# An encoder layer by Strassen-like products: w_ada blocks in turn, weights asked for ahead, other rings, and right output columns kept on chip

## The chip, the cores and the metric

One core of a Trainium2 chip (8 cores) runs the kernel. Its engines are TensorE (PE; its weight loads are PEld), VectorE (DVE), ScalarE (ACT), GpSimd (POOL) and SyncE (SP). Transfers are issued here by SP and POOL (a few at the start by ACT) and carried out by 16 DMA engines. The metric is the device time of one execution in microseconds; lower is better.

## What is computed

One layer of a bidirectional encoder on x of 1024 x 2048 (float32):

```python
mod = jax.nn.silu(c) @ w_ada + b_ada                 # w_ada 2048 x 6144
shift, scale, gate = jnp.split(mod, 3, axis=-1)
h = rmsnorm(x, pre_g) * (1.0 + scale[:, None]) + shift[:, None]
proj = h @ w_in                                      # 2048 x 4608
q, k, v, gate_a, u, gate_p = jnp.split(proj, SPLIT_POINTS, axis=-1)
y_a = windowed_gqa(q, k, v, rel_table, sink) * jax.nn.silu(gate_a)
y_p = multiscale_pool(u, w_pool_grp, pool_scale) * jax.nn.silu(gate_p)
g = jax.nn.sigmoid(h @ w_merge + b_merge)            # 2048 x 4096
g_a, g_p = jnp.split(g, N_BRANCHES, axis=-1)
merged = g_a * (y_a @ w_br_attn) + g_p * (y_p @ w_br_pool)
o = merged @ w_out                                   # 2048 x 2048
return x + gate[:, None] * rmsnorm(o, post_g)
```

## The kernel before

**Products.** A float32 factor is split into a high part (ACT, line 91) and a low part (DVE, line 92), and a product is three matmuls: high by high, high by low, low by high. Blocks of 256 weight columns by 1024 rows of x are multiplied by a seven-product scheme of the Strassen-Winograd kind (`strassen`, line 199). One such unit, a *pair* below, has seven steps; with four row tiles a step is 12 matmuls of 128x512, with two (in the ramp) it is 6. `product` issues the matmuls (line 223), `prep` splits the weights, DVE forms the sums of weights in `raw` tiles, and ACT and DVE take the banks X, Z and V out. Raw weights come as two tiles of a ring of four, loaded by `load_raws` (line 178) at the opening of the pair's generator. `run` (line 306) drives one pair through its steps; the last step of a pair is issued at step 2 of the next one (`flush`), and *side steps* from a queue are hung between the steps (`placed`, line 94: behind the last matmul and the last low part).

**Order.** The program is built by a framework that keeps dependencies, places tiles in memory and fixes the order of every engine's instructions ahead of the run; each engine and each DMA queue then runs its own list in that order, waiting where something is not there yet.

**Stages.** (1) *Start* (lines 331 to 533): x is loaded and its rows normed and transposed; w_ada is used in blocks of 256 columns. Blocks 0 and 1 are loaded by SP and 2 and 3 by POOL (`ada_slots`, line 407; 16 tiles of 256 KB each), their column sums are formed on PE (`modulation`, lines 415 and 427), and each fills one row tile of the moving operands (`fill_steps`, line 478). (2) *Ramp* (lines 535 to 555): six pairs with the first two row tiles, then the same six with the other two; blocks 2 and 3 are side steps from numbers 4 and 15, their fills from 12 and 27. (3) *First pass* (`pass1`, line 559): the remaining pairs with the first half of K. The first 19 carry side steps at 4 of 7 steps: the rest of w_ada (`modulation_steps`, `gate_step`), sums of w_out's tiles for the last stage (`weight_sums`), the gate row by eight row sums (`gate_row`, line 599), and last the lines of the attention bias (`bias_lines`, line 583), which end in a 2 MB copy in DRAM on POOL's queue. The other nine carry x's second half at 5 of 7 steps (`x_step`, line 698): load by POOL, scaling by ACT (line 686), transposes by PE (line 692), and more weight sums. x and weight sums share a ring of eight tiles (`x_tile`, line 679). (4) *Second pass*: 34 pairs with the second half of K, with attention and pooling at their side. (5) *Branches* (line 979): 16 pairs. (6) *Last stage* (lines 1050 to 1344): merged @ w_out by the same scheme in four blocks of seven products of 48 matmuls (line 1102). Blocks 0 and 1 use the first half of K and store their results to `po_d`; 2 and 3 use the second half, load them back and add. Block 2 (left columns of each half) stores its weighed results to `o_d`, which the end loads again as `orow`; in `finish_rows` (line 1285) a row's scale is formed and 32 tiles are written out, nine of them by scaling on ACT and a transfer that adds x in place, the others by one DVE instruction each (line 1298).

```python
        queue(tiles[kc], w_ada[...])                                # ada_slots, 411
        raws = raws or load_raws(w, n0, row0, js)                   # strassen, 209
        side.insert(100, bias_lines)                                # 665: the list has 75 entries
```

Of the kernel before, what the change touches and what calls it, by code (L numbers as in the profile page):

```python
# [42 lines left out]
def encoder_layer(ctx: ExitStack, tc: tile.TileContext, x, c, table, w_ada, b_ada, pre_g,  # L43
# [95 lines left out]
    o_d = dram.tile([S, D // 2], F32, name="o_d")  # L139
# [59 lines left out]
    def strassen(w, n0, row0, js, op, finish, part=None, raws=None, swap=False):  # L199
# [9 lines left out]
        raws = raws or load_raws(w, n0, row0, js)  # L209
# [89 lines left out]
    late, evs = [], [None]  # L299
# [6 lines left out]
    def run(gen, side=None, every=(0, 2, 4, 6), at=None, then=None):  # L306
# [224 lines left out]
    for tag in SEEDED:  # L531
        hi = op["B11"][0][0]
        nc.tensor.matmul(bank(tag, "OPEN"), hi[:, 0:P], hi, start=True, stop=True)

    def ramp_pair(jj, i, parts, at):
# [3 lines left out]
        if ahead < 2 * RAMP:  # L539
            raws.append(load_raws(*weight_of(ORDER[ahead % RAMP]), 0, ((0, 1), (2, 3))[ahead // RAMP]))  # L540
        run(strassen(w, n0, 0, (2 * jj, 2 * jj + 1), op, to_dram(dst), parts, raws[jj * RAMP + i]),
            side, range(7), at)

    parts = {}
# [52 lines left out]
    gsum = {}  # L597

    def gate_row(n):
        if n < 8:  # L600
            gsum[n] = bank("at")
            nc.tensor.matmul(gsum[n][0:1, 0:256], ones, gacc[:, n * 256:(n + 1) * 256],
                             start=True, stop=True)
        n -= 1
        if n < 0:
            return
        sl = slice(n * 256, (n + 1) * 256)
        grow = gp.tile([1, 3, 256], F32, tag="grow", name=uid("grow"))
        side_load(grow[:, 0, :], b_ada[0:1, 2 * D + n * 256:2 * D + (n + 1) * 256])
        side_load(grow[:, 1, :], post_g[0:1, sl])  # L610
        add(grow[:, 2, :], gsum.pop(n)[0:1, 0:256], grow[:, 0, :])
        nc.vector.tensor_tensor(grow[:, 2, :], grow[:, 2, :], grow[:, 1, :], ALU.mult)
        side_store(pg_d[:, sl], grow[:, 2, :])
# [50 lines left out]
    side.extend(lambda n=n: gate_row(n) for n in range(9))  # L664
    side.insert(100, bias_lines)
# [13 lines left out]
    def x_tile():  # L679
        return sp.tile([P, 512], F32, tag="xt2", name=uid("xt"), bufs=8)  # L680
# [17 lines left out]
    def x_step(n):  # L698
        if n < 2 * NB:
            held[n] = fetch_x(n // 2, n % 2)  # L700
        if n >= 2:
            turn_x((n - 2) // 2, n % 2, held.pop(n - 2))

    steps = [lambda n=n: x_step(n) for n in range(2 * NB + 2)]
    steps += [lambda k=k, s=s: modulate((nc.scalar, nc.vector)[s], h[k][s], k) for k in h for s in range(2)]
    side = deque(with_sums(steps, 2, 4, range(8, 16), x_tile))
# [340 lines left out]
    def mslot(name, dt=F32, shape=(P, 512)):  # L1047
# [8 lines left out]
    queue = deque((q, w) for q in range(4) for _, w in ORDERS[q])  # L1056
# [20 lines left out]
    def prep_wo():  # L1077
# [4 lines left out]
        for src in loaded.popleft():  # L1082
            if not queue and not loaded:
# [29 lines left out]
    def out_sums(q, banks, fetch_op):  # L1113

        i = q % 2
        bx, bz = banks

        def copied(name, ps):
            for t in range(4):
                r = ev.tile([P, 512], F32, tag="pv", name=uid("c"), bufs=2)  # L1120
                nc.scalar.activation(r, ps[t], AF.Copy)
                store(at_rows(po_d, name, t, i), r)

        def summed(name, r, ps):
            for t in range(4):
                add(r[t], ps[t], r[t])
                store(at_rows(po_d, name, t, i), r[t])
# [6 lines left out]
        u2 = four("ev")  # L1134
# [7 lines left out]
        u3 = four("gt")  # L1142
# [41 lines left out]
    def put_later(n):  # L1184
# [4 lines left out]
        for j in range(KS):  # L1189
            t = mslot("lm")  # L1190
# [19 lines left out]
    for j in range(KS):  # L1210
        put(op, "T2", j, mt2[j])
        sub(m_t[2 * j, 0], mt2[j], m_t[2 * j, 0])
    out_sums(0, new_banks(0), first_fetch)
    out_sums(1, new_banks(1), put_later)
# [8 lines left out]
    parts, rows_x, rows_o = {}, {}, {}  # L1223

    def fetch_sums(i, blk):
        parts[blk] = [mslot("po") for _ in range(4)]
        for t in range(4):
            load(parts[blk][t], at_rows(po_d, blk, t, i))
# [6 lines left out]
    def weigh(i, blk, r):  # L1235
        nc.vector.tensor_tensor(r, r, pgrow[int(blk[0]) - 1][:, i * 512:(i + 1) * 512], ALU.mult)

    def take(i, blk, ps, r):

        for t in range(4):  # L1240
            add(r[t], ps[t], r[t])
            squares(i, blk, t, r[t])
            weigh(i, blk, r[t])
            if i == 0:
                store(at_rows(o_d, blk, t, 0), r[t])
# [4 lines left out]

    bx, bz = new_banks(2)
    fetch_sums(0, "12")
    product("B11", bx, True)
    for t in range(4):
        nc.scalar.activation(bz[t], bx[t], AF.Copy)
    fetch_sums(0, "11")
    product("T2", bz, False)
    seeded(bz, parts["12"])
    fetch_sums(0, "22")
    product("B21", bx, False)  # L1260
    take(0, "11", bx, parts["11"])
    product("T3", bz, False)
    seeded(bz, parts["22"])
    fetch_sums(0, "21")
    product("T1", bx, True)
    take(0, "22", bx, parts["22"])
    product("T4", bz, False)
    take(0, "21", bz, parts["21"])
    product("B22", bx, False)
    take(0, "12", bx, parts["12"])  # L1270

    def by_dma(half, t, n):
        return n in (0, 2) if half == 0 else n == 0 and t == 0

    def fetch_rows(half, t):
        si = half * 4 + t
        rows_x[si] = [None if by_dma(half, t, n) else slot("xr", F32) for n in range(4)]
        rows_o[si] = [slot("orow", F32) for _ in range(2)]
        for n in range(2):
# [103 lines left out]
```

## Time and profile before

| | |
|---|---|
| median of 3 runs | 2195.38 us (2192.98 to 2196.26) |
| the profiled execution | 2197.48 us, its span 2195.6 us |
| mean granted TensorE clock | 0.985 |
| HBM read, written | 329.92 MB, 142.63 MB |
| DMA packets' share of 16 engines, SP's queue | 53.9% |
| the same, POOL's queue | 11.6% |

The span runs from the first to the last instruction of one profiled execution, and all durations below are from it. A row of an engine's timeline has start and duration in us, the engine, the line of the kernel, the operation, output <- inputs, and how many instructions are merged; in brackets stands the idle time before it and what ended that. A row of a stretch has busy time and count of PE and PEld (and of DVE, ACT and POOL where no line is chosen), then granted clock, share of the DMA engines and GB/s. SPq, POOLq are the queues' issuing instructions.

### The profile page before, as it was taken

To read this page: it belongs to the slowest core of one execution; us is meant where nothing else is said; L and a number is where in the kernel's file an instruction comes from. 1 tells how busy PE (TensorE), PEld (TensorE's weight loads), DVE (VectorE), ACT (ScalarE), POOL (GpSimd) and SP (SyncE) were. 2 spreads that over 40 slices of the span, in tenths; PEclk is the share of its full clock that TensorE was granted. 3 is DMA by queue.
4 is the path that set the end of the run, shared out by engine and by line. 5 is a ranking of instruction groups with operands and counts; after the bars stand their busy time and mean duration, and the time that the engine had idled before them with its cause. 6 is when DMAs were issued, how large, how long until landed. Compare 5 with 4: busy or idle time off the path is not lost. (4 is left out here: it accounts for less than half of the span.)

```text
span 2195.6 us, 29101 instructions
## 1 busy us (share of the span) xinstructions
PE 2102.8 (96%) x9613; PEld 1714.9 (78%) x9613; DVE 1500.3 (68%) x2699; ACT 1088.8 (50%) x2015; POOL 179.8 (8%) x388
## 2 busy tenths in 40 slices
PE   5799999999999789999999999999999999999996
PEld 3478888877777568888888888788888788788884
DVE  6478777766444596777776777865867977655557
ACT  5464443433345554677667433333645645545344
POOL 2201232221201400000000000000000000000001
PEclk9799999999999999999999999999999999999998
DMA  9658778875445855554654576675754646898498
GB/s 332 220 201 271 254 271 271 270 264 172 146 140 156 289 197 188 174 175 149 204 171 144 180 227 202 206 240 173 243 165 160 218 134 203 258 330 265 156 316 270
DMA packets 280392, 472.42 MB, mean 215 GB/s; under 512 B 25898, under 2 KB 122258, under 8 KB 280240
## 3 DMA queue, kind: packets, MB, share of 16 engines
q1 hardware_dynamic: 252880, 386.22, 53.9%
q0 software_dynamic: 27024, 84.28, 11.6%
q8 instruction: 76, 1.25, 0.2%
q14 instruction: 76, 0.62, 0.1%
q10 hardware_dynamic: 336, 0.06, 0.0%
HBM read 329.92 MB, written 142.63 MB: 215 GB/s over the span
## 5 line engine op out<-in xcount | busy, mean ns | idle before, releaser
L91 ACT ACTIVATE whi<-raw 128x512 fp32r<-128x512 f32 (+1 forms) x540 | 320.8, 600 | 507.6 <-PE Z L223 235.0
L92 DVE TENSOR_TENSOR wlo<-raw,whi 128x512 fp32r<-128x512 f32 (+1 forms) x540 | 348.8, 652 | 148.9 <-PE Z L223 110.6
L102 DVE TENSOR_TENSOR raw<-raw,raw 128x512 f32<-128x512 f32 x78 | 54.0, 692 | 117.7 <-DMA raw<-in_w_merge_dram 68.4
L92 DVE TENSOR_TENSOR wlo<-wr,whi 128x512 fp32r<-128x512 f32 x112 | 76.3, 688 | 63.4 <-ACT whi L91 63.4
L91 ACT ACTIVATE whi<-wr 128x512 fp32r<-128x512 f32 x112 | 69.6, 627 | 98.9 <-PE OUT L1102 94.3
L223 PE MATMUL V<-T3h,whi 128*128 128x512 f32 x336 | 95.1, 400 | 6.0 <-DVE u L102 5.9
L223 PE MATMUL X<-B11h,whi 128*128 128x512 f32 x336 | 93.2, 395 | 7.0 <-ACT B11h L91 4.0
L223 PE MATMUL Z<-T2h,whi 128*128 128x512 f32 x336 | 93.4, 396 | 4.4 <-ACT whi L91 3.7
L223 PE MATMUL Z<-T2h,wlo 128*128 128x512 f32 x336 | 92.8, 394 | 3.4 <-DVE wlo L92 3.4
L223 PE MATMUL X<-B11l,whi 128*128 128x512 f32 x336 | 92.7, 392 | 2.5 <-DVE B11l L92 2.5
L223 PE MATMUL Z<-T1h,whi 128*128 128x512 f32 x336 | 94.1, 395 | 1.0 <-ACT T1h L91 0.8
L223 PE MATMUL V<-T3h,wlo 128*128 128x512 f32 x336 | 92.4, 395 | 1.6 <-DVE wlo L92 1.6
L223 PE MATMUL Z<-B22h,whi 128*128 128x512 f32 x336 | 92.3, 393 | 1.4 <-ACT u L272 1.4
L223 PE MATMUL V<-T4h,whi 128*128 128x512 f32 x336 | 92.3, 392 | 0.7 <-ACT T4h L91 0.7
L223 PE MATMUL V<-T3l,whi 128*128 128x512 f32 x336 | 92.9, 395 | 0.0
L223 PE MATMUL Z<-B22h,wlo 128*128 128x512 f32 x336 | 91.0, 390 | 1.9 <-DVE wlo L92 1.9
L223 PE MATMUL Z<-T2l,whi 128*128 128x512 f32 x336 | 92.7, 394 | 0.0
L223 PE MATMUL X<-B21h,wlo 128*128 128x512 f32 x336 | 91.1, 390 | 1.2 <-DVE wlo L92 1.2
L223 PE MATMUL Z<-T1l,whi 128*128 128x512 f32 x336 | 92.2, 392 | 0.0
L223 PE MATMUL X<-B11h,wlo 128*128 128x512 f32 x336 | 91.8, 391 | 0.0
L223 PE MATMUL V<-T4h,wlo 128*128 128x512 f32 x336 | 91.1, 390 | 0.5 <-DVE wlo L92 0.5
L223 PE MATMUL X<-B21h,whi 128*128 128x512 f32 x336 | 91.6, 392 | 0.0
(360 smaller groups left out, 5034.4 us busy)
## 6 DMA issues: line engine op xcount, KB each, us to landing
part<-part_d SPq DMA_DIRECT2D x136, 256.0 KB, 4.6
raw<-in_w_merge_dram SPq DMA_DIRECT2D x64, 512.0 KB, 5.0
raw<-in_w_in_dram SPq DMA_DIRECT2D x60, 512.0 KB, 4.4
ada<-in_w_ada_dram POOLq DMA_DIRECT2D x96, 256.0 KB, 5.7
proj_d<-part SPq DMA_DIRECT2D x68, 256.0 KB, 2.2
gada<-in_w_ada_dram POOLq DMA_DIRECT2D x32, 512.0 KB, 6.1
gt<-proj_d SPq DMA_DIRECT2D x64, 256.0 KB, 3.6
wr<-ws_d SPq DMA_DIRECT2D x32, 512.0 KB, 5.7
```

Source lines behind the costliest of these rows:

```text
L91: nc.scalar.activation(hi, src, AF.Copy)
L92: return nc.vector.tensor_tensor(lo, src, f32(hi), ALU.subtract)
L102: (eng or nc.vector).tensor_tensor(o, a, b, ALU.add)
L223: last_mm[0] = nc.tensor.matmul(ps, w_[:, i], op[mov][j][m_], start=fresh and i == 0 and n == 0, stop=i == nj - 1 and n == 2, skip_group_c ...
```

## The change

1. *Start.* A small POOL instruction (`mark`) reads tile 13 of block 1, and the loads of blocks 2 and 3 are put behind it on POOL. Ten opening matmuls (five a bank, before one a bank) stand between the sums of block 1 and its fill, before at the end of both fills. In the ramp, blocks 2 and 3 are side steps from 10 and 19 (one a step, and every second step), the fill of block 2 from 14.
2. *Weights.* `run` asks for the raw weights of the next full pair at its step 3 (`fetch_weights`) from a list of all pairs to come; `strassen` takes what was loaded.
3. *Gate row and bias.* The gate's sums are 16 products of one column each, then one transpose and two DVE instructions; its vectors are loaded at once, with the bias lines, at step 9 of the first part of the first pass. That part has 18 pairs, so x comes in ten.
4. *Rings.* x and weight sums have four tiles each of their own; x is transposed three steps after its load instead of two.
5. *Last stage.* The blocks run in the order 0, 1, 3, 2. Block 1 keeps its 16 result tiles on chip, in the ring that held the merged input, and block 3 adds to them and keeps them to the end; the tiles through which the second operand is read move to another ring. `o_d`, the adding transfers and the second trip of the right columns fall away. Partial results of block 0 and x come by POOL's queue. The products T4 and T1 of the final block run row by row as B22 did, the weights of the last but one product have slots of their own, rows are finished from T4 on, and the seed of B22 is added before it.

```diff
-    late, evs = [], [None]
+    late, evs, fetched, wanted_w = [], [None], deque(), deque()
+
+    def fetch_weights():
+        if wanted_w:
+            fetched.append(load_raws(*wanted_w.popleft(), range(4)))
...
-        raws = raws or load_raws(w, n0, row0, js)
+        raws = raws or fetched.popleft()
...
+            if i == 3 and ahead:
+                fetch_weights()
...
-    ada += [ada_slots(m, side_load) for m in (2, 3)]
+    mark = const.tile([P, 1], F32, name="mark")
+    come = ada[1][KT - 3][:, 0, 0:1]
+    with tc.issue_after(nc.gpsimd.tensor_tensor(mark, come, come, ALU.add).ins):
+        ada += [ada_slots(m, side_load) for m in (2, 3)]
     for m in range(2):
         all_of(modulation(m, ada[m]))
+        if m == 1:
+            for tag in SEEDED * 5:
+                hi = op["B11"][0][0]
+                nc.tensor.matmul(bank(tag, "OPEN"), hi[:, 0:P], hi, start=True, stop=True)
         all_of(fill_steps(m))
     claim((2, 3))
     side = deque([lambda: None] * (7 * RAMP))
-    for m, g0, f0 in ((2, 4, 12), (3, 15, 27)):
+    for m, g0, f0 in ((2, 10, 14), (3, 19, 27)):
         for n, f in enumerate(modulation(m, ada[m])):
-            side[g0 + 2 * n] = f
+            side[g0 + (m - 1) * n] = f
...
+    wanted_w.extend((*weight_of(n0), 0) for n0 in ORDER[RAMP:])
+    wanted_w.extend((*weight_of(n0), HALF * P) for n0 in ORDER)
+    wanted_w.extend((w, n * 256, 0) for w in (w_ba, w_bp) for n in range(8))
...
+    def gate_columns():
+        pg = bank("at")
+        for k in range(KT):
+            nc.tensor.matmul(pg[:, k:k + 1], gacc[:, k * P:(k + 1) * P], ones, start=True, stop=True)
+        nc.vector.tensor_copy(gcol, pg[:, 0:KT])
...
-    side.extend(lambda n=n: gate_row(n) for n in range(9))
-    side.insert(100, bias_lines)
+    side.extend((gate_columns, gate_row))
+    side.insert(9, lambda: (fetch_gate_row(), bias_lines()))
...
-        return sp.tile([P, 512], F32, tag="xt2", name=uid("xt"), bufs=8)
+        return sp.tile([P, 512], F32, tag="xt2", name=uid("xt"), bufs=4)
+
+    def sum_tile():
+        return sp.tile([P, 512], F32, tag="ws2", name=uid("wsum"), bufs=4)
...
+    BLOCKS = (0, 1, 3, 2)
...
-            if not queue and not loaded:
+            if len(queue) + len(loaded) == 1:
                 hi, lo = slot("whi"), slot("wlo")
...
-            t = mslot("lm")
+            t = ev.tile([P, 512], F32, tag=("gt", "ev")[n % 2], name=uid("lm"), bufs=4)
...
-    out_sums(1, new_banks(1), put_later)
+    out_sums(1, new_banks(1), put_later, kept)
...
     def finish_rows(half, t):
...
-            if by_dma(half, t, n):
-                nc.scalar.activation(o_[n], o_[n], AF.Copy, scale=s_[:, 2:3])
-                nc.gpsimd.dma_start(o_[n], x[at], accum_op=ALU.add)
...
+        for n in (1, 3, 2, 0):
+            o_ = (last, kept)[n % 2][f"{n // 2 + 1}{half + 1}"][t]
+            nc.vector.scalar_tensor_tensor(o_, o_, s_[:, 2:3], rows_x[si][n], op0=ALU.mult, op1=ALU.add)
+            store(out[si * P:(si + 1) * P, n * 512:(n + 1) * 512], o_)
...
-    product("T4", bx, False)
...
+    product("T4", bx, False, by_rows=True)
+    for t in range(2):
+        fetch_rows(1, t)
     for t in range(4):
+        squares(0, "21", t, bx[t])
+        weigh(0, "21", last["21"][t], bx[t])
+        finish_rows(0, t)
+    product("T1", bz, False, by_rows=True)
+    for t in range(2, 4):
         fetch_rows(1, t)
...
+        squares(0, "22", t, bz[t])
+        weigh(0, "22", last["22"][t], bz[t])
+        add(bz[t], bz[t], last["12"][t])
     product("B22", bz, False, by_rows=True)
     for t in range(4):
...
+        squares(0, "12", t, bz[t])
+        weigh(0, "12", last["12"][t], bz[t])
         finish_rows(1, t)
```

More of the change, by code (lines that the diff above doesn't have):

```diff
@@ L304, in flush, with run @@
             next(late.pop())
-    def run(gen, side=None, every=(0, 2, 4, 6), at=None, then=None):
+    def run(gen, side=None, every=(0, 2, 4, 6), at=None, then=None, ahead=True):
         for i in range(7):
@@ L595, in bias_lines, with gate_row, fetch_gate_row @@
               bass.AP(line_d.tensor, line_d.offset, [[LINE, NH], [0, P], [1, LINE]]))
[L597 to L613, printed above, removed]
+    grow = gp.tile([KT, 4, P], F32, name="grow")
+    gcol = gp.tile([P, KT], F32, name="gcol")
+    def gate_columns():
[3 more added lines that the diff above has]
+        nc.vector.tensor_copy(gcol, pg[:, 0:KT])
+    def gate_row():
+        pt = bank("at")
+        nc.tensor.transpose(pt[0:KT, 0:P], gcol, ident)
+        add(grow[:, 2], pt[0:KT, 0:P], grow[:, 0])
+        nc.vector.tensor_tensor(grow[:, 3], grow[:, 2], grow[:, 1], ALU.mult)
+        side_store(pg_d.rearrange("a (r p) -> (a r) p", p=P), grow[:, 3])
+    def fetch_gate_row():
+        side_load(grow[:, 0], b_ada[0, 2 * D:3 * D].rearrange("(r p) -> r p", p=P))
+        side_load(grow[:, 1], post_g[0].rearrange("(r p) -> r p", p=P))
     def weight_sums(n, tile_):
@@ L1055, in encoder_layer @@
     SETS = (("sc", "sc", "at", "at"), ("mm", "mm", *SEEDED))
-    queue = deque((q, w) for q in range(4) for _, w in ORDERS[q])
+    queue = deque((q, w) for n, q in enumerate(BLOCKS) for _, w in ORDERS[n])
     loaded, ready = deque(), deque()
@@ L1111, in at_rows, with out_sums, tiles, done @@
         return d[r0:r0 + P, n0:n0 + 512]
[L1113 to L1115 removed]
+    def out_sums(i, banks, fetch_op, keep=None):
         bx, bz = banks
+        def tiles(tag):
+            return four(tag) if keep is None else [mslot("po") for _ in range(4)]
+        def done(name, t, r):
+            if keep is None:
+                store(at_rows(po_d, name, t, i), r)
+            else:
+                keep.setdefault(name, []).append(r)
         def copied(name, ps):
             for t in range(4):
[L1120 removed]
+                r = ev.tile([P, 512], F32, tag="pv", name=uid("c"), bufs=2) if keep is None else mslot("po")
                 nc.scalar.activation(r, ps[t], AF.Copy)
[L1122 removed]
+                done(name, t, r)
         def summed(name, r, ps):
@@ L1133, in out_sums @@
         product("T2", bz, False)
-        u2 = four("ev")
+        u2 = tiles("ev")
         for t in range(4):
@@ L1141, in out_sums @@
         product("T3", bz, False)
-        u3 = four("gt")
+        u3 = tiles("gt")
         for t in range(4):
@@ L1249, in seeded, with opening, ev_tile @@
             add(r[t], ps[t], r[t])
-    bx, bz = new_banks(2)
[L1252 to L1261, printed above, removed]
+    def opening(banks, r12, then):
+        bx, bz = banks
+        product("B11", bx, True)
+        for t in range(4):
+            nc.scalar.activation(bz[t], bx[t], AF.Copy)
+        then()
+        product("T2", bz, False)
+        seeded(bz, r12)
+        product("B21", bx, False)
+    def ev_tile(tag):
+        return ev.tile([P, 512], F32, tag=tag, name=uid("po"), bufs=4)
+    bx, bz = new_banks(2)
+    opening((bx, bz), kept["12"], lambda: None)
+    take(1, "11", bx, kept["11"])
     product("T3", bz, False)
-    seeded(bz, parts["22"])
-    fetch_sums(0, "21")
+    seeded(bz, kept["22"])
+    fetch_sums("12", lambda: ev_tile("ev"))
+    fetch_sums("11", lambda: ev_tile("gt"))
     product("T1", bx, True)
-    take(0, "22", bx, parts["22"])
+    take(1, "22", bx, kept["22"])
     product("T4", bz, False)
-    take(0, "21", bz, parts["21"])
+    take(1, "21", bz, kept["21"])
     product("B22", bx, False)
-    take(0, "12", bx, parts["12"])
-    def by_dma(half, t, n):
-        return n in (0, 2) if half == 0 else n == 0 and t == 0
+    take(1, "12", bx, kept["12"])
     def fetch_rows(half, t):
         si = half * 4 + t
-        rows_x[si] = [None if by_dma(half, t, n) else slot("xr", F32) for n in range(4)]
-        rows_o[si] = [slot("orow", F32) for _ in range(2)]
-        for n in range(2):
-            load(rows_o[si][n], o_d[si * P:(si + 1) * P, n * 512:(n + 1) * 512])
+        rows_x[si] = [slot("xr", F32) for _ in range(4)]
         for n in range(4):
-            if rows_x[si][n] is not None:
-                load(rows_x[si][n], x[si * P:(si + 1) * P, n * 512:(n + 1) * 512])
+            side_load(rows_x[si][n], x[si * P:(si + 1) * P, n * 512:(n + 1) * 512])
     def finish_rows(half, t):
```

74 lines of the change are left out of this document (22 added, 52 removed).

## The prediction

> **What bounds the kernel now.** I read the page first: its busy times and TensorE's row of tenths over 40 slices.
>
> ```profile
> span 2195.6 us, 29101 instructions
> PE 2102.8 (96%) x9613; PEld 1714.9 (78%) x9613; DVE 1500.3 (68%) x2699; ACT 1088.8 (50%) x2015; POOL 179.8 (8%) x388
> ...
> PE   5799999999999789999999999999999999999996
> ```
>
> TensorE bounds nearly all of it. It is short of full in three places: the first two slices, the slices around 760 us and the last one. A busy share hides smaller holes, so I counted the products' own matmuls (line 223) in stretches, and took the pitch of a full product from the chain of waits.
>
> ```profile
> 1588.30 2.72 PE V L223 x12
> 640.00:680.00 40.00, 40.00 (x178) 33.12 (x177) 1.00 0.37 111
> 440.00:640.00 200.00, 189.59 (x812) 153.17 (x811) 0.98 0.57 186
> 680.00:840.00 160.00, 134.06 (x544) 102.38 (x543) 0.97 0.68 226
> ```
>
> Twelve matmuls in 2.72 us are 0.227 us each; an undisturbed stretch has 178 in 40 us. At that rate 440 to 640 should hold 890 and 680 to 840 should hold 712. Missing are 78 (17.7 us) and 168 (38 us). These two holes, the start and the end are what the change can win; elsewhere TensorE runs at its pitch or the change doesn't reach, and what it saves there on other engines or in transfers is worth nothing.
>
> **The start.** Block 1 of w_ada (16 tiles, SP queue) shares the transfers with blocks 2 and 3 on POOL.
>
> ```profile
> 0.74 22.02 SPq L355 DMA_DIRECT2D xt<-in_x_dram  x32
> 36.74 23.82 SPq L411 DMA_DIRECT2D ada<-in_w_ada_dram  x16
> 39.22 5.95 POOL L411 DMA_DIRECT2D ada<-in_w_ada_dram  x8 [0.61 <-PE GEMV L427]
> 50.97 0.69 DVE L92 TENSOR_TENSOR B22l<-XT,B22h 128x512 fp32r<-128x512 f32 x1
> 68.22 0.42 DVE L432 COPY acc<-GEMV 128x256 f32<-128x256 f32 x1 [14.52 <-PE GEMV L427]
> xt<-in_x_dram SPq DMA_DIRECT2D x32, 256.0 KB, 5.4
> 79.34 1.22 PE L223 MATMUL Z<-T2h,whi 128*128 128x512 f32 x2 [0.67 <-ACT Z L249]
> 84.20 0.91 PE L223 MATMUL X<-B21h,whi 128*128 128x512 f32 x2
> ```
>
> Alone, x tiles of the same 256 KB went out every 22.02/32 = 0.69 us; the 16 tiles of block 1 took 23.82/16 = 1.49 us each. With blocks 2 and 3 held back behind the mark, 16 x 0.69 = 11 us of issue and 5.4 us to land put the last tile at 53 us and the copy of its sums near 54, now 68.2. DVE has finished the operands of block 0 at 51.7 and then stands until those sums come, so nothing else is late before 54: the first products come **14 us** earlier. Bounds: 10 (the raw weights issued behind block 1 are late, or what follows) and 15 (DVE is then the limit). Blocks 2 and 3 now start near 51; their 32 issues at 0.69 us end some 22 us later, and later still beside the stores: near 80. The side steps that need them move from 4 and 15 to 10 and 19; at 6 x 0.227 = 1.36 us a step after a start near 64 that is 78 and 90, and each block is taken over four steps. They just fit; if not, PE stands in order before such a step.
>
> The ten opening matmuls stand in PE's order between the sums and the first product, where it waits for operands anyway. From 79.34 to 84.20, 11 matmuls ran at 0.44 us each, twice the pitch; at 0.227 they would save 2.4 us. The ten could warm the clock in that gap: from 0 to 2.4, I take 1.5.
>
> The Trainium skill, "TensorE: Matmul & The Clock Gate", section "What's actually happening", says that the full clock comes after a busy window of about 3.4 us, and that the windows run free of the kernel. By that rule ten matmuls of 0.44 us fill one window or none, and this term would be 2.4 or 0; the 0.44 agrees with its half clock.
>
> **The gate row.** Eight sums of two matmuls over 256 columns become 16 of one column and one transpose.
>
> ```profile
> 532.71 1.07 PE L223 MATMUL X<-B21h,wlo 128*128 128x512 f32 x4
> 533.71 0.59 PE L602 MATMUL b<-gacc,ones 128*1 128x256 f32 x2
> 534.24 1.20 PE L223 MATMUL V<-T4h,whi 128*128 128x512 f32 x4
> 535.27 1.08 PE L223 MATMUL V<-T4l,whi 128*128 128x512 f32 x4
> 41.54 1.08 PE L396 MATMUL PM<-ones,acc 128*128 128x1 f32 x8
> ```
>
> From 532.71 to 535.27 pass 2.56 us for eight matmuls worth 1.82: one group costs 0.74, eight cost 5.9. The new sums have the form of line 396, 1.08 us for eight: 2.2 for 16, and about 0.5 for the transpose. Saved **3.2** (2 to 4). The small loads on POOL become two and come early; the bias lines take their memset, two loads, matmuls, copy and two stores with them to step 9, at the same cost on PE. The first pass is one pair shorter and the second one longer.
>
> **Weights ahead.** Two stalls stand in the same hole.
>
> ```profile
> 474.67 1.28 DVE L578 SCALAR_TENSOR_TENSOR gacc<-gada,sc,gacc 128x1024 f32<-128x1024 f32 x1 [3.03 <-DMA gada<-in_w_ada_dram]
> 480.55 0.69 DVE L105 TENSOR_TENSOR ws<-raw 128x512 f32<-128x512 f32 x1 [3.39 <-DMA raw<-in_w_merge_dram]
> 481.89 2.07 PE L223 MATMUL V<-T3h,whi 128*128 128x512 f32 x4 [4.04 <-DVE u L102]
> 606.80 0.69 DVE L105 TENSOR_TENSOR ws<-raw 128x512 f32<-128x512 f32 x1 [7.88 <-DMA raw<-in_w_merge_dram]
> 608.15 1.19 PE L223 MATMUL V<-T3h,whi 128*128 128x512 f32 x4 [1.87 <-DVE u L102]
> SPq L189 <- DVE wlo L92: 127.3, 119, 9.0
> ```
>
> DVE runs in order: it waits for raw weights, its read of V behind that is late, and PE stands 4.04 and 1.87 us. The four matmuls at 481.89 then take 2.07 us where those at 608.15 take 1.19; at half clock for three such groups the first stall costs 2.6 more. Loads asked for at step 3 of the pair before stand half a pair further ahead and cover the waits for raw, not the 3.03 for gada. Of 8.5 us I take **7** (2 to 8.5).
>
> **The x stretch** is the large term.
>
> ```profile
> 590.20 1.13 POOL L594 DMA_DIRECT2D bias_d<-line_d  x1 [1.55 <-DMA line_d<-bl]
> 591.32 1.12 POOL L685 DMA_DIRECT2D xt<-in_x_dram  x2
> L686 ACT ACTIVATE xt<-xt,rstd x16: 703/714/722, 697.9 to 741.1; 128x512 f32<-128x512 f32 x16
> L105 DVE TENSOR_TENSOR xt<-xt,xt 128x512 f32<-128x512 f32 x24 | 16.4, 689 | 22.2 <-DMA xt<-in_w_out_dram 21.6 <-issue 0.6
> L692 PE MATMUL b<-ident,xt 128*128 128x128 f32 x64 | 10.5, 290 | 6.6 <-ACT xt L686 6.6
> 200.00:240.00 40.00, 40.00 (x178) 32.99 (x177) 31.37 (x45) 18.06 (x30) 14.91 (x28) 1.00 0.90 303
> ```
>
> The first x tiles are asked for at 591.32, yet ACT scales the first at 697.9, five pairs of work later: the order of its instructions, fixed when the program is built, has x that late. The one unusual thing ahead of it is the 2 MB copy of the bias lines on the same queue, and I read this as an order made for a very long copy. The 38 steps are then squeezed into some 90 us instead of eight pairs (150 us), with one ring for x and the weight sums, so that DVE stands 21.6 us for tiles of the sums and PE behind it. Of the 38 us missing, the 64 transposes are needed work (at most 10.5, some 8 at their pitch): 30 us are waits. In the change the copy stands at step 9 of the first pass, x has a ring of its own, its transpose comes a step later, and eight of ten pairs carry it. I leave 5 for waits on DVE that remain: **25** won (12 to 30).
>
> The price is that the side steps behind the copy in the first pass may be put late and squeezed there: about 100 us at a step each quarter of a pair (4.8 us) are some 21 steps. They hold no PE work, and from 200 to 240 DVE (31.37 of 40 us) carried a dense side with no matmul missing; I take **5** lost (0 to 25, nearly what the squeeze costs now).
>
> **The end.** The stores and loads of partial results that go were beside a PE at its pitch: nothing. The 16 tiles kept on chip take a ring whose old tenants were read a block before. After the last matmul 21.3 us remain.
>
> ```profile
> 2173.94 0.39 PE L1102 MATMUL OUT<-whi,B22l 128*128 128x512 f32 x1
> 2146.76 1.28 DVE L105 TENSOR_TENSOR po<-po,OUT 128x512 f32<-128x512 f32 x2
> 2181.47 1.42 DVE L1298 SCALAR_TENSOR_TENSOR orow<-orow,st,xr 128x512 f32<-128x512 f32 x2
> 2182.80 1.41 DVE L1298 SCALAR_TENSOR_TENSOR po<-po,st,xr 128x512 f32<-128x512 f32 x2
> 2188.72 1.09 SPq L1300 DMA_DIRECT2D out_dram<-po  x2
> 2163.97 9.80 DMA orow<-in_x_dram
> ```
>
> DVE ends at 2184.2 and is the limit from the sums of T3 (2148) on. The change gives it all 32 final products (0.665 us each by the last rows: 21.3), 12 weighings and 4 sums at 0.60 (9.6), 8 splits (4.8) and small ones (2): 37.7 us from 2148 is 2185.7, or 1.5 later. But SP, which was held by the accumulating transfers (9.80), issues its last store 5 us behind DVE now and would follow within 0.5. Won **4**; from 9 (T4 by rows lets DVE start earlier) to a loss of 3. The loss has two places: the seeds of B22 stand on DVE behind the final products of the first half, and T4 by rows wants its four weight tiles within a quarter of a product. The loads of x and of the last sums go to POOL's queue, a product ahead of need: hidden, but see rival 5.
>
> **Sum**, from the profiled execution (2197.5 with what lies around its span, 2.1 over the median of the runs shown): 14 + 1.5 + 3.2 + 7 + 25 + 4 - 5 = 49.7. 2197.5 - 49.7 = 2147.8, on the median's scale **2146**.
>
> **Rivals.**
>
> 1. The squeeze only moves: the first pass pays 25, not 5. For it: same copy, same queue. Against it: no PE work in those steps. 2166.
> 2. The change doesn't unbunch x, because the copy isn't what puts it late. For it: no row shows the cause of the order. Then neither the 25 nor the 5 come: 2166 too.
> 3. All covers hold: start 17, gate 4, raw 8.5, x 30, end 9, nothing lost: 68.5, so 2127.
> 4. Slower: SP runs in order, and the loads of the next pair now stand ahead of this pair's later stores. They wait for raw tiles that the pair before frees (127.3 us over 119 waits now, 9.0 the longest). Where the ring of results runs dry behind such a wait, every full pair pays (28 + 34 + 16 = 78); from 49.7/78 = 0.64 us a pair it is slower. At 0.9: 2216. Against it: by step 3 those tiles have just been freed.
> 5. POOL's queue is late for the last two blocks.
>
> ```profile
> xt<-in_x_dram POOLq DMA_DIRECT2D x16, 256.0 KB, 6.4
> ```
>
> A tile of x lands in 6.4 us by POOL and in 5.4 by SP. If each of the eight rows of output stands that 1 us longer behind its x, with DVE the limit, the end is 8 us later: 2154. Against it: x is asked for a product ahead. The Trainium skill, "SBUF — State Buffer", section "SBUF: two separate sides", lets some of DVE's instructions lock GpSimd out of the port through which it writes its transfers' descriptors; no row here shows that by itself.
>
> **Chances.** Forecast 0.54, its own range 2134 to 2158; rivals 1 and 2 together 0.25; 3 0.12; 4 0.05; 5 0.04. The range 2124 to 2174 takes in 1, 2, 3 and 5 and leaves out 4 and the far ends of the sums. 0.2% is about what a measurement of this kernel can tell from no change. Faster 0.93, within it 0.02, slower 0.05.
>
> **What would show it.** Right: the copy of block 1's sums near 54 and steady products from about 64; gate matmuls of one column; no wait of PE for DVE's read of V in the first pass; ACT's first scaling of x within 10 us of its load; line 223 at nearly its full count there; the last store within 1 us of DVE's last product. Wrong: DVE waits for ada or gada in a cluster some 100 us after the bias copy; x's scaling still far behind its load; longer waits of SP before raw, with matmuls missing in every pair.

## The result, and the profile after

| | before | after |
|---|---|---|
| median | 2194.89 us (2192.98 to 2196.26, 4 runs) | 2175.72 us (2168.21 to 2179.62, 4 runs) |
| span of the profiled execution | 2195.6 us | 2172.8 us |

The ratio is 0.9909, with a 95% interval of 0.9881 to 0.9937. The change is faster, by 19 us where 49 were forecast, and it lies 2 us outside the forecast's range (2124 to 2174). The page of the changed kernel, with span, busy times and tenths of the span in 40 slices:

```profile
span 2172.8 us, 29010 instructions
...
PE   5999999889989999999999999999999999999997
...
GB/s 329 263 228 300 210 154 201 333 325 235 184 222 243 137 151 206 160 168 170 182 173 140 190 225 217 214 236 170 231 168 162 213 138 205 253 262 227 98 213 252
```

The hole around 760 us is gone and the second slice is full. New thin slices stand between 380 and 490 us, where the traffic is now as high as in the first slice (333 and 325 GB/s), and one around 625 us. The products' matmuls in five stretches, after, with columns as in the prediction:

```profile
200.00:360.00 160.00, 156.16 (x686) 128.15 (x685) 1.00 0.56 185
360.00:440.00 80.00, 67.09 (x281) 54.38 (x280) 0.94 0.97 332
440.00:520.00 80.00, 72.86 (x310) 58.58 (x310) 0.98 0.92 319
520.00:680.00 160.00, 146.34 (x599) 114.25 (x598) 0.96 0.62 200
680.00:840.00 160.00, 160.00 (x708) 132.51 (x707) 1.00 0.52 168
```

The same view of the kernel before (its last stretch stands in the prediction, with 544):

```profile
360.00:440.00 80.00, 78.42 (x345) 64.30 (x344) 1.00 0.81 268
440.00:520.00 80.00, 75.96 (x324) 62.32 (x323) 0.96 0.78 260
```

An undisturbed stretch of 80 us holds 356. From 360 to 440 us after has 281 where before had 345, and its transfers are at 0.97 of the engines. From 680 to 840 us it has 708 of 712. So the change closed one hole and opened another.

To put this in microseconds I cut both spans at the start of pairs (the first matmul X<-B11h,whi of a pair). The pairs are counted from 1: 1 to 12 are the ramp, 13 to 40 the first pass, pair 15 is the third of it, pairs 28 to 43 hold the x stretch and the opening of the second pass, and pair 90 is the last of the branches.

| stretch | before | after | difference | forecast |
|---|---|---|---|---|
| to pair 15 | 242.4 | 226.1 | -16.3 | -15.5 (start, opening matmuls) |
| pair 15 to 28 | 258.5 | 279.1 | **+20.6** | -2 (weights ahead -7, squeeze +5) |
| pair 28 to 44 | 351.1 | 329.3 | -21.8 | -28.2 (x -25, gate row -3.2) |
| pair 44 to 90 | 991.2 | 990.2 | -1.0 | 0 |
| pair 90 to the end | 352.4 | 348.2 | -4.2 | -4 |

The start and the end came out near their forecast. 29 us are missing, 22.6 in the first pass and 6.4 in the x stretch, and the other three stretches bring 2 more than forecast. (The weights' 7 stand whole in the second row, though the smaller of their two stalls, 1.87 us at 608.15, lies in the third.) The timeline of POOL, after, at the copy of the bias lines:

```profile
243.10 1.10 POOL L605 DMA_DIRECT2D bias_d<-line_d  x1 [2.23 <-DMA line_d<-bl]
...
351.00 1.06 POOL L455 DMA_DIRECT2D ada<-in_w_ada_dram  x2 [68.57 <-DVE acc L459]
```

POOL issues the copy at 243.10 and goes on loading ada tiles until its ring is full; then it waits 68.57 us for DVE to use one. DVE does so from 349.42, 106 us behind the copy:

```profile
349.42 1.28 DVE L459 SCALAR_TENSOR_TENSOR acc<-ada,sc,acc 128x1024 f32<-128x1024 f32 x1
```

In the kernel before x was scaled 107.7 us behind the same copy (590.2 to 697.9). DVE has no idle time in front of that sum at 349.42: its list of instructions simply comes to it that late. Yet the copy lands fast, as its transfer's row says (KB, us from issue to landing):

```profile
bias_d<-line_d POOLq DMA_DIRECT2D x1, 2048.0 KB, 16.7
```

What the delay costs stands on TensorE's timeline, after:

```profile
391.01 1.19 PE L222 MATMUL V<-T3h,whi 128*128 128x512 f32 x4 [3.27 <-DVE u L102]
...
407.17 3.54 PE L401 MATMUL PM<-ones,acc 128*128 128x1 f32 x16 [4.98 <-DVE acc L459]
410.57 2.05 PE L222 MATMUL V<-T4h,whi 128*128 128x512 f32 x4
412.43 1.91 PE L222 MATMUL V<-T4l,whi 128*128 128x512 f32 x4
414.13 1.91 PE L222 MATMUL V<-T4h,wlo 128*128 128x512 f32 x4
415.84 1.45 PE L222 MATMUL Z<-T1h,whi 128*128 128x512 f32 x4
417.12 1.08 PE L222 MATMUL Z<-T1l,whi 128*128 128x512 f32 x4
```

TensorE stands 4.98 us before line 401, the column sums that end a block of modulation, because DVE is not yet through the squeezed sums. The 16 matmuls then take 3.40 us from start to start, in run 1 below 1.70, and the next 16 of the products 6.55 us instead of 3.63: 4.6 us are lost again. Before the stand of 3.27 us at 391, DVE had three of the sums and two sums of w_out's tiles in its list (385.40 to 390.28) ahead of its read of V.

### The profile page after: what moved, and what is told of

Read it like the earlier page. It is cut to its first block, busy times and chain, and to the rows that moved or that the text cites. A ratio compares the mean times of both kernels' runs of the same rounds, so it can differ in the third digit from the quotient of the medians.

```text
span 2172.8 us, 29010 instructions
## 1 busy us (share of the span) xinstructions
PE 2101.9 (97%) x9638; PEld 1725.6 (79%) x9638; DVE 1501.2 (69%) x2695; ACT 1081.7 (50%) x2006; POOL 187.7 (9%) x407
## 4 chain that ended last, share of the span: by engine, by line
PE 78%; DMA 12%; DVE 6%; issue 2%; ACT 1%; POOL 1%; SPq 0%; DVEq 0%; ACTq 0%; POOLq 0%
PE Z L222 26%; PE V L222 18%; PE X L222 18%; PE OUT L1119 11%; DMA ada<-in_w_ada_dram 2%; DMA gada<-in_w_ada_dram 2%; DMA xt<-in_x_dram 1%; DMA raw<-in_w_merge_dram 1%; DVE wlo L92 1%; DMA raw<-in_w_in_dram 1%; DVE po L1316 1%; DMA gt<-proj_d 1%; PE PT L851 1%; DMA lm<-m_d 1%; PE GEMV L432 1%
## 5 line engine op out<-in xcount | busy, mean ns | idle before, releaser
L222 PE MATMUL V<-T4l,whi 128*128 128x512 f32 x336 | 91.9, 393 | 0.0
```

Source lines behind the costliest of these rows:

```text
L222: last_mm[0] = nc.tensor.matmul(ps, w_[:, i], op[mov][j][m_], start=fresh and i == 0 and n == 0, stop=i == nj - 1 and n == 2, skip_group_c ...
```

## The experiments

Theory A says that the 2 MB copy on POOL's queue has the steps behind it put about 100 us late in the order that is fixed when the program is built; the late steps are then squeezed, many of them into little time, and the first pass now pays for this where x paid before. The rivals are that the density of the steps, the loads of weights ahead, the rings or POOL's queue on the chip are the cause. All ratios are to the kernel before, measured again beside each run.

**1. The copy on ScalarE's queue** (the base of most later runs).

```diff
-        side_store(bias_d.rearrange("h (p l) -> h p l", l=LINE),
+        nc.scalar.dma_start(bias_d.rearrange("h (p l) -> h p l", l=LINE),
```

> The changed kernel with one line changed: the 2 MB copy of the bias lines is issued from ScalarE's queue and no longer from POOL's, where the small loads of the steps beside the products are issued. Theory A (the copy has whatever is issued behind it on its queue put about 100 us late in the order, and squeezed): the sums for modulation of the first pass run four to a pair from its start, the stalls of TensorE of 3.43 and 5.14 us near 387 and 402 us and the one of 4.09 us near 483 us go with the matmuls at half clock behind them, 15 to 22 us in all: 2153 to 2161 us. Theory B (the first pass loses its time to the density of the steps or to the loads of weights ahead, wherever the copy stands): 2172 to 2178 us. The wait of ScalarE for x, some 13 us near 520 to 680 us, stays by both.

Measured: 2149.97 us, ratio 0.9784 (0.9768 to 0.9801), 26 us faster than the change by one line, and 3 us under the range that theory A gave. Pairs 15 to 28 take 259.4 us instead of 279.1. The products' matmuls in the stretches of this run, and its sums for modulation:

```profile
360.00:440.00 80.00, 78.46 (x347) 64.65 (x346) 1.00 0.85 280
440.00:520.00 80.00, 79.81 (x353) 65.76 (x352) 1.00 0.75 250
520.00:680.00 160.00, 146.16 (x601) 114.18 (x600) 0.96 0.64 208
```

```profile
L459 DVE SCALAR_TENSOR_TENSOR acc<-ada,sc,acc x30: 1274/1280/1287, 201.0 to 352.8; 128x1024 f32<-128x1024 f32 x30
```

The hole from 360 to 520 us is gone (700 matmuls against 591), and the sums end at 352.8 us; in the changed kernel, whose row is the next, they end at 405.7. From 520 to 680 us nothing changed (601 against 599), as expected.

```profile
L459 DVE SCALAR_TENSOR_TENSOR acc<-ada,sc,acc x30: 1274/1279/1287, 200.5 to 405.7; 128x1024 f32<-128x1024 f32 x30
```

**2. The copy last, still on POOL's queue.**

```diff
-    side.insert(9, lambda: (fetch_gate_row(), bias_lines()))
+    side.insert(9, fetch_gate_row)
+    side.append(bias_lines)
```

> The changed kernel with the bias lines and their copy as the last of the side steps of the first pass instead of the tenth; the copy stays on POOL's queue. Theory A: the first pass is freed as in the run before (15 to 22 us won) and the loads of x, which now follow the copy, are put late and squeezed as in the kernel before, which costs 15 to 25 us there: 2170 to 2185 us, with ScalarE's first scaling of x about 100 us behind the copy. Theory B (the copy has no part in the order): within 3 us of the changed kernel, and x where it was.

Measured: 2169.95 us, 0.9873 (0.9859 to 0.9888). Pairs 15 to 28 take 251.6 us, the least of all runs, and pairs 28 to 44 take 354.0, as much as in the kernel before. From 680 to 840 us its products count 594 of 712:

```profile
680.00:840.00 160.00, 143.28 (x594) 114.82 (x593) 0.95 0.60 198
```

The copy is issued at 539.14 us, and ScalarE's first scaling of x comes at 645.7, 106.6 us behind it. The hole follows the copy. That is theory A, with both prices of one mechanism seen in one kernel.

**3. The kernel before, with the copy on ScalarE's queue** (the same line).

> The kernel before with the one line changed: the copy of the bias lines on ScalarE's queue. Theory A: x is scaled within some 20 us of its load instead of 107.7 us behind the copy, and most of the 38 us of products missing from 680 to 840 us comes back: won 15 to 25 us, 2170 to 2180 us. Theory B (x is late and squeezed for another reason): 2193 to 2197 us.

Measured: 2176.17 us, 0.9905 (0.9891 to 0.9919). The loads and the scalings of x in this run, with first and last start:

```profile
L685 POOL DMA_DIRECT2D xt<-in_x_dram x16: 536/536/579, 587.8 to 657.9; - x16
L686 ACT ACTIVATE xt<-xt,rstd x16: 702/722/725, 591.4 to 664.0; 128x512 f32<-128x512 f32 x16
```

The first scaling comes 3.6 us behind its load instead of 106.6. One line in the old kernel brings as much as the whole change (0.9905 against 0.9909). Pairs 28 to 44 take 336.9 us, 14 less than before; the change as a whole has 329.3 there. The profiled execution of this run is its slowest, 5 us over the median, so its stretches may understate the gain.

**4. The change without weights ahead.**

```diff
-        raws = raws or fetched.popleft()
+        raws = raws or load_raws(w, n0, row0, js)
...
-            if i == 3 and ahead:
-                fetch_weights()
```

> The changed kernel without the loads of raw weights a pair ahead: each pair asks for its own at its start, as in the kernel before. If the loads ahead win what the prediction gave them (7 us, in the two stalls of the first pass alone): 2180 to 2184 us. If they win nothing now, because the steps beside the products set DVE's lateness: 2173 to 2178 us. If they cost time by standing ahead of the stores on SP's queue: 2160 to 2172 us, with every pair shorter.

Measured: 2174.66 us, 0.9902 (0.9883 to 0.9921): no difference from the change. That could be the squeeze hiding a gain, so run 10 repeats it on the base.

**5. x by SP's queue**, on the base.

```diff
-        side_load(xt, x[si * P:(si + 1) * P, c0:c0 + 512])
+        load(xt, x[si * P:(si + 1) * P, c0:c0 + 512])
```

> The copy on ScalarE's queue as in the first of these runs (the base of these four, 2150 us), and the loads of x in the second pass issued from SP's queue, where the weights and the partial results go, instead of POOL's. Theory C (ScalarE stands 22.8 us for tiles of x, and TensorE's transposes behind it, because a load of x is issued in order behind stores of weight sums on POOL's queue, and these wait for DVE): ScalarE's wait for x falls below 8 us, the stalls of TensorE of 1.17 and 4.35 us near 598 and 615 us go with the half clock behind them, 6 to 12 us won: 2138 to 2144 us. Theory D (x waits because too many transfers are under way there, or for its ring of four tiles): the wait stays, 2147 to 2153 us.

Measured: 2150.43 us, 0.9786 (0.9768 to 0.9804), the base's time. ScalarE's wait for x, which was 22.8 us in the base, grew:

```profile
  ACT xt L702: 28.6, 8
```

Theory C falls: POOL's queue is not what delays x.

**6. One ring of eight, x transposed two steps behind its load**, on the base (the lines of change 4 undone).

> The base with the ring as in the kernel before: one ring of eight tiles for x and the weight sums, x transposed two steps behind its load instead of three. If the rings of their own are what freed the stretch (a term of 25 us in the prediction): DVE waits for tiles of the weight sums again and it is 10 to 25 us slower, 2160 to 2175 us. If the stretch was freed by where the copy stands, and the ring has no part in it: 2147 to 2153 us. If four tiles for x are too few: faster than the base by some us.

Measured: 2150.65 us, 0.9789 (0.9771 to 0.9806); pairs 28 to 44 take 328.9 us as in the base. DVE no longer waits for tiles of the weight sums with either ring (its groups in this run: busy, mean ns, idle before):

```profile
L105 DVE TENSOR_TENSOR wsum<-wsum,wsum 128x512 f32<-128x512 f32 x25 | 17.1, 684 | 0.1
```

The 21.6 us of such waits in the kernel before came from the squeeze, not from the shared ring.

**7. The first rows' final products behind the seeds of B22**, on the base.

```diff
         weigh(0, "21", last["21"][t], bx[t])
-        finish_rows(0, t)
...
         add(bz[t], bz[t], last["12"][t])
+    for t in range(4):
+        finish_rows(0, t)
```

> The base with the final products of the first half of the rows emitted behind the seeds of the last product (its sums with T1) instead of ahead of them. Theory E (DVE is the limit from T3's sums to the end, so TensorE's stand of 4.51 us before B22 costs nothing): the stand goes, the last matmul ends some 6 to 8 us earlier, and the time stays within 2 us of the base, 2148 to 2152 us. Theory F (the stand itself puts the end off): 4 to 7 us faster, 2143 to 2146 us.

Measured: 2149.23 us, 0.9778 (0.9762 to 0.9795), the base's time within its error. The last matmul is now 18.2 us ahead of the span's end (2145.2), in the base 11.5; TensorE's last row and DVE's last row of this run:

```profile
2126.98 0.39 PE L1119 MATMUL OUT<-whi,B22l 128*128 128x512 f32 x1
```

```profile
2137.18 2.74 DVE L1316 SCALAR_TENSOR_TENSOR po<-po,st,xr 128x512 f32<-128x512 f32 x4
```

TensorE is finished 6.7 us sooner, counted from the end. DVE's last product ends 342.4 us after the start of pair 90 (1797.5 us), in the base 342.9 (2146.7 after 1803.8), so DVE is where it was: theory E.

**8. No mark**, on the base (blocks 2 and 3 free to load at once).

```diff
-    with tc.issue_after(nc.gpsimd.tensor_tensor(mark, come, come, ALU.add).ins):
-        ada += [ada_slots(m, side_load) for m in (2, 3)]
+    ada += [ada_slots(m, side_load) for m in (2, 3)]
```

> The base without the mark: the loads of blocks 2 and 3 of w_ada are free to start at once, as in the kernel before; the opening matmuls, and the steps of these blocks put later beside the products, stay. If the mark is what starts the products earlier (14 us by the prediction, 16 in the traces of before and after): 12 to 16 us slower, 2162 to 2166 us. If it is the later steps or the opening matmuls: 2148 to 2154 us.

Measured: 2165.73 us, 0.9851 (0.9833 to 0.987), 16 us slower than the base by the medians and 10 by the profiled spans. DVE's copy of block 1's sums in this run:

```profile
67.36 0.42 DVE L437 COPY acc<-GEMV 128x256 f32<-128x256 f32 x1 [13.75 <-PE GEMV L432]
```

In the base it starts at 56.45. Pair 15 starts 10.9 us later too (237.5 against 226.6). So much is the mark's. The other 5 us of the start lie between that copy and the first steady product (`Z<-T2h,whi`), which comes 11.1 us behind the copy in the kernel before (68.22 to 79.34) and 7.0 in this run; from there to pair 15 both take 163.1 us. TensorE waits less there for the operands of block 1's fill. First the kernel before, then this run:

```profile
73.32 0.79 PE L223 MATMUL X<-B11h,whi 128*128 128x512 f32 x1 [4.01 <-ACT B11h L91]
77.02 0.79 PE L223 MATMUL X<-B11l,whi 128*128 128x512 f32 x1 [2.49 <-DVE B11l L92]
```

```profile
70.97 0.79 PE L222 MATMUL X<-B11h,whi 128*128 128x512 f32 x1 [2.52 <-ACT B11h L91]
74.39 1.22 PE L222 MATMUL Z<-T2h,whi 128*128 128x512 f32 x2 [0.67 <-ACT Z L248]
```

Which of the other edits at the start shortened the fill, no run shows.

**9. x scaled a step later**, on the base: `x_step` loads tile n, scales tile n - 1 and transposes tile n - 3.

> The base (the changed kernel with the copy on ScalarE's queue, 2150 us) with ScalarE's scaling of a tile of x one step behind its load instead of in the same step; ring, queue and transposes as in the base. Theory G (the rest of the stretch of x is lost because ScalarE, which runs in order, meets the scaling before the tile has landed, and so is late for the operands that TensorE waits for): ScalarE's wait for x falls from 22.8 to below 6 us, and the stalls of 1.17 and 4.35 us near 598 and 615 us go: 6 to 12 us faster, 2138 to 2144 us. If the loads are simply too late, wherever the scaling stands: within 3 us of the base.

Measured: 2151.98 us, 0.9811 (0.9788 to 0.9835). ScalarE still waits 23.6 us for x, so the run moved the step in the text and not the wait; theory G got no test from it.

**10. No weights ahead**, on the base.

> The base without the loads of raw weights a pair ahead. In the changed kernel itself leaving them out made no difference (2174.7 against 2175.7 us), but there the squeezed sums kept DVE late anyway. If they win the 7 us of the prediction once the squeeze is gone: 2154 to 2158 us, with DVE's waits for raw of 3 to 8 us near 470 to 600 us and a stand of TensorE behind them. If the two stalls that they were to cover came from the steps and not from the loads: 2147 to 2153 us.

Measured: 2147.45 us, 0.9783 (0.9761 to 0.9805), no slower than the base. The issues of raw weights show why; first the kernel before, where pairs start at 455.9 and 475.0 us, then the base, at 447.4 and 466.4 (SP's timeline):

```profile
450.64 0.38 SPq L189 DMA_DIRECT2D raw<-in_w_merge_dram  x1
458.24 0.49 SPq L189 DMA_DIRECT2D raw<-in_w_merge_dram  x1
469.86 0.38 SPq L189 DMA_DIRECT2D raw<-in_w_merge_dram  x1
482.47 0.38 SPq L189 DMA_DIRECT2D raw<-in_w_merge_dram  x1
```

```profile
440.49 0.38 SPq L188 DMA_DIRECT2D raw<-in_w_merge_dram  x1
448.47 0.38 SPq L188 DMA_DIRECT2D raw<-in_w_merge_dram  x1
461.79 0.38 SPq L188 DMA_DIRECT2D raw<-in_w_merge_dram  x1
470.07 0.38 SPq L188 DMA_DIRECT2D raw<-in_w_merge_dram  x1
```

Against the pair's start the loads went from -5.3, +2.3, -5.1 and +7.5 us to -6.9, +1.1, -4.6 and +3.7: at most 4 us earlier and not half a pair. Pair 27 took 22.9 us without the loads ahead and 19.5 in the base, but 23.1 in run 12, which has them. The ring has four raw tiles and a pair uses two; a request made earlier seems to wait there for a tile that the pair before still holds: SP's waits for DVE before these loads, 127.3 us in the kernel before, are 163.8 in the base (its row: us, times, longest). No run gave the ring more.

```profile
SPq L188 <- DVE wlo L92: 163.8, 130, 11.2
```

**11. The old gate row**, on the base.

> The base with the gate row computed as in the kernel before: eight sums of two matmuls of 256 columns and nine steps with two small loads and a store each, in place of sixteen matmuls of one column and a transpose in two steps. By the prediction's count on TensorE 3.2 us (2 to 4) slower: 2152 to 2154 us. If the nine steps cost more than their matmuls, because they wait for their small loads or push the steps of x a pair further back: 2155 to 2162 us. If they cost nothing beside the rest: 2148 to 2151 us.

Measured: 2159.49 us, 0.9834 (0.9809 to 0.9858), the profiled span 2152.1. It is slower than the base, by 9.5 us in the medians and 1.9 in the spans (the profiled execution is the fastest of its five), and I cannot say more exactly how much. Its matmuls on PE, against those of the changed kernel (busy us, mean ns):

```profile
L613 PE MATMUL b<-gacc,ones 128*1 128x256 f32 x16 | 4.7, 377 | 0.0
```

```profile
L614 PE MATMUL b<-ones,gacc 128*128 128x1 f32 x32 | 4.1, 263 | 0.0
L619 PE MATMUL b<-ident,gcol 128*16 128x128 f32 x1 | 0.4, 415 | 0.0
```

Sixteen products of one column are 32 instructions in the trace, so TensorE's own work is 4.5 us against 4.7. Pairs 28 to 44 take 329.3 us against 328.9: what the old gate row costs lies elsewhere, and is not found.

**12. Seven eighths of the copy on POOL's queue, one on ScalarE's**, otherwise as the change.

```diff
-        side_store(bias_d.rearrange("h (p l) -> h p l", l=LINE),
-              bass.AP(line_d.tensor, line_d.offset, [[LINE, NH], [0, P], [1, LINE]]))
+        for eng, h0, h1 in ((nc.gpsimd, 0, 7), (nc.scalar, 7, 8)):
+            eng.dma_start(bias_d[h0:h1].rearrange("h (p l) -> h p l", l=LINE),
+                          bass.AP(line_d.tensor, line_d.offset + h0 * LINE, [[LINE, h1 - h0], [0, P], [1, LINE]]))
```

> The changed kernel with seven of the eight heads of the bias copy still on POOL's queue, at the same place in it, and the eighth head on ScalarE's. In the program as built so, DVE's order has the sums for modulation four to a pair again, though POOL's queue carries almost the whole copy. Theory A1 (what costs is the order of the instructions, which is fixed when the program is built; the copy on the chip's queue costs nothing): the squeeze is gone as with the whole copy moved, 2147 to 2154 us. Theory A2 (on the chip, loads issued behind the copy on POOL's queue come late): DVE and TensorE wait for ada tiles after about 243 us, 2160 to 2176 us.

Measured: 2151.98 us, 0.9797 (0.9773 to 0.9821), the base's time. The transfer on POOL's queue and the sums of this run:

```profile
bias_d<-line_d POOLq DMA_DIRECT2D x1, 1792.0 KB, 16.5
```

```profile
L459 DVE SCALAR_TENSOR_TENSOR acc<-ada,sc,acc x30: 1273/1279/1285, 200.5 to 350.6; 128x1024 f32<-128x1024 f32 x30
```

Nearly the whole copy stood in the same queue at the same place (243.76 us) and took 16.5 us; the sums ran early all the same. So the copy on the chip's queue costs nothing that can be measured, and the order of the instructions costs the 20 us. Why the order allows some 107 us behind the whole copy and nothing behind this one is not settled.

**13. Copy on ScalarE's queue, bias lines last, rows later** (the edits of 1, 2 and 7).

> The changed kernel with what the runs so far point to: the copy on ScalarE's queue and the bias lines as the last side steps of the first pass (so that no matmul of the first pass waits for their loads, which cost 6 us near 237 us in some executions of the base), and the final products of the first half of the rows behind the seeds of the last product. If the first pass then runs at its pitch from pair 12 on as it did with the bias lines last (478.7 us at the 28th pair against 486.0 in the base): 2141 to 2148 us. If what is saved there is lost again where x follows: 2148 to 2153 us.

Measured: 2151.13 us, 0.979 (0.9767 to 0.9813). The first pass is at its best again (252.2 us from pair 15 to 28), but pairs 28 to 44 take 331.7 and the time is the base's: a gain of some us in one stretch disappears in the spread and in the x stretch. The best kernels are the one-line base and its neighbours, at 0.978 of before.

## Why the prediction was right or wrong

**The step that failed** is the price of the copy's new place: "They hold no PE work, and from 200 to 240 DVE (31.37 of 40 us) carried a dense side with no matmul missing; I take 5 lost (0 to 25, nearly what the squeeze costs now)". Both halves of the reason were wrong. The steps do hold PE work: each block of modulation ends in 16 matmul instructions of line 401 that wait for DVE's last sum (4.98 us at 407). And DVE's busy share says nothing of such a wait: from 349 to 410 us DVE is busy 45.5 of 61 us in the changed kernel and 44.3 in run 1, yet TensorE is busy 51.5 there against all 61. What differs is what stands where in the lists: the sums of 106 us come at once, ahead of the read of V (3.27 us) and of the column sums. They also wait for their tiles seven times, 5.3 us in all from 373 to 400, with the transfers at 0.91 of the engines against 0.85; that is the prediction's own first sign of being wrong. The cost was 279.1 - 259.4 = 19.7 us by run 1, and 279.1 - 251.6 = 27.5 by run 2, where the bias lines' own work and waits are out of the stretch too. The mechanism was in the prediction as its first rival ("the first pass pays 25, not 5", 2166); it had the right cause and was given too small a chance (0.25 together with the second), because I argued about what the steps hold and did not follow the chain from sums to column sums. It still falls 10 us short of 2175.7: the weights ahead, the gate row and the x stretch came smaller too.

**Why x was late** was read rightly: "this as an order made for a very long copy". Runs 2 and 3 show it for x and run 1 for the first pass, and run 12 shows, in the first pass, that it is the order alone. The second rival falls.

**The x stretch** was sized 25 and, with the gate row's 3.2, brought 21.8. Most or all of it is the copy's place: 14.2 us by run 3, and 24.7 by run 2, which has every other edit of the change and takes 354.0 us against 329.3 (the bias lines' own work included). The rings, which the prediction named beside it, have no part (run 6), and rings and gate row undone singly on the base cost nothing in this stretch (328.9 and 329.3 against 328.9). Why run 3 has 8 us less of it than the change is not found; its slow profiled execution may be a part. ScalarE's waits for x remain, 23.2 us in the changed kernel:

```profile
L702 ACT ACTIVATE xt<-xt,rstd 128x512 f32<-128x512 f32 x16 | 11.4, 717 | 23.2 <-DMA xt<-in_x_dram 23.2
```

Most of them cost nothing by themselves: in run 5 they grew to 28.6 us and the stretch took 326.5. TensorE's one long stand from 520 to 700 us is 4.66 us before 639.19, for a result that ScalarE copied at 638.56, right behind a scaling that had waited 5.21 us. The queue is not the cause of the waits (run 5); what is stays open.

**The start**, 14 and 1.5, came out at 16.3: the mark is its main cause (run 8). That the sum fits so well is in part luck. The copy of block 1's sums came at 56.40 and not near 54, 11.8 us earlier instead of 14, and the rest is the shorter fill behind it, which the prediction does not have. The share of the opening matmuls was wrong. They ran from 46.39 to 52.4, among the sums of block 1, and not in the gap; the clock of TensorE in four stretches after (all engines, then clock, DMA share, GB/s):

```profile
52.00:58.00 6.00, 5.44 (x56) 2.97 (x55) 2.52 (x9) 1.19 (x4) 3.92 (x6) 1.00 1.10 352
58.00:62.00 4.00, 1.62 (x5) 0.78 (x5) 3.96 (x8) 4.00 (x7) 3.27 (x6) 0.95 1.03 346
62.00:68.00 6.00, 5.33 (x13) 3.90 (x13) 4.52 (x9) 3.09 (x8) 5.78 (x9) 0.50 1.01 344
68.00:72.00 4.00, 4.00 (x18) 3.29 (x17) 2.81 (x8) 2.23 (x5) 3.91 (x6) 0.95 1.01 345
```

The clock was full before the first products, TensorE then stood 2.52 us for the fill and was busy for only 1.62 of the 4 us from 58, and from 62 to 68 us the granted clock was 0.50, as it was from 76 to 84 us in the kernel before. The prediction's other outcome for this term, nothing, is what happened.

**Weights ahead**, 7, brought nothing that can be measured (runs 4 and 10). In the stall that it was to cover DVE still waited for raw (2.11 us at 485.07) and TensorE for DVE (3.92 us at 487.02) in the changed kernel. The step that failed is that loads asked for at step 3 "stand half a pair further ahead".

**The gate row**, 3.2, was 4.7 - 4.5 = 0.2 us of TensorE's work: the eight instructions of line 396 that I counted as eight columns are four. Run 11 says that the old form costs more than that, by a way that is not found.

**The end**, 4, brought 4.2, and for the stated reason: DVE is the limit from T3's sums on, and SP's last issue ends 0.4 us behind DVE's last product (2169.59 after 2169.23). The size is in part luck: the terms as written add up to 3 (5 less 0.5 less 1.5). DVE's last product came 3.6 us later after the start of pair 90 instead of 1.5 (344.6 against 341.0), but the span now ends 3.6 us behind it, before 11.4. The stand before B22, which the prediction had named as a place of loss, came (4.35 us) and cost nothing (run 7), because TensorE was not what the end waited for.

The fourth rival (a slower kernel by loads ahead of stores) did not come: SP does wait longer before raw (179.0 us in the changed kernel against 127.3), but pairs 44 to 90 take 990.2 us against 991.2.

## What to carry to other kernels

When a step is moved past a long transfer or in front of one, ask what the build's order puts behind it and follow that chain to the engine that bounds the kernel; the stall may be in the list of instructions and in no queue. A cheap test is to send the suspect from another queue, or to cut it in two, before redesigning what stands around it. A wait that looks like a ring too small, or weights too late, may be the echo of steps squeezed together elsewhere.

## What the runs showed that was not expected

A stand of TensorE costs more than its length: after 4.98 us, the next 12 matmuls took 5.3 us (410.57 to 415.84) where 2.7 is the pitch, and a stand of only 2.52 us was followed by six microseconds at a granted clock of 0.50. The Trainium skill, "TensorE: Matmul & The Clock Gate", section "Why this matters for your kernels", advises against gaps of over about 3 us; here the clock fell with no gap that long: 2.52 us, behind a microsecond of one-column matmuls and ahead of 4 us in which TensorE was busy for 1.62.

The same first pass can lose 6 us or not. In the base's profiled execution TensorE stood for a small load of the bias lines, and behind it four matmuls of the products took up to 1.9 us instead of 1.07 (granted clock 0.84 from 244 to 252 us):

```profile
241.10 1.02 PE L601 MATMUL b<-oh,tab 33*8 33x512 f32 x2 [3.23 <-DMA oh<-in_onehot_dram]
```

Pair 15 took 25.15 us there and 20.62 us in run 9, whose first pass has the same steps. Differences of a few us between single profiled executions are within that.
